# Constant products at phase boundaries, modulation products moved to the mixer's end, and interleaved Strassen products in a two-layer diffusion trunk on one core

## Chip, cores and metric

The kernel runs on one core of one Trainium2 chip (trn2). The metric is the device time of one execution in microseconds (us). The engines are named as in the profile: PE is TensorE's matmul queue and PEld its weight loads, DVE is VectorE, ACT is ScalarE, POOL is GpSimd and SP is SyncE, which issues the DMAs.

## What is computed

The trunk has two layers on 640 tokens (128 of a context, 512 of a latent grid). Each layer is a SwiGLU channel mixer, a token mixer (layer 0 a bidirectional gated recurrence, RG-LRU; layer 1 a multi-scale pooling), and a second SwiGLU, each between two RMS norms and with a shift, a scale and a gate that come from a conditioning vector by a product with `mod_w`:

```python
def _layer(x, mod, l, norm_g, ffn_w1, ffn_w3, ffn_w2, mixer):
    sh1, sc1, g1, sh2, sc2, g2, sh3, sc3, g3 = jnp.split(mod[:, None, :].astype(x.dtype), N_MOD, axis=-1)
    h = _modulate(_rmsnorm(x, norm_g[l, 0]), sh1, sc1)
    x = x + 0.5 * g1 * _rmsnorm(_swiglu(h, ffn_w1[l, 0], ffn_w3[l, 0], ffn_w2[l, 0]), norm_g[l, 1])
    h = _modulate(_rmsnorm(x, norm_g[l, 2]), sh2, sc2)
    y, st = mixer(h)
    x = x + g2 * _rmsnorm(y, norm_g[l, 3])
    h = _modulate(_rmsnorm(x, norm_g[l, 4]), sh3, sc3)
    x = x + 0.5 * g3 * _rmsnorm(_swiglu(h, ffn_w1[l, 1], ffn_w3[l, 1], ffn_w2[l, 1]), norm_g[l, 5])
    return x, st
```

The width is 1024, the SwiGLU's inner width 2816. In the recurrence, `r` and `i` are sigmoids of products of the convolved input with 128x128 blocks, `a = exp(-8 r softplus(-lam))`, and two scans run over the tokens, one in each direction; their sum times the gelu of a gate goes through `w_out`.

## The kernel before

**Numbers.** All large products are of f32 data. Each factor is split into a high and a low part of type fp32r, and one product is three passes (low·high, high·low, high·high). The split costs two instructions for each piece: an ACT copy (L136, L207) and a DVE subtraction (L137, L208); `split` takes another engine for the subtraction if it is given one.

**Seven products.** A SwiGLU's up-projections (`ffn_u`, `ffn_v`, 11 pairs of 128-column matrices, called b here, of which u and v belong to `w1` and `w3`) are done Strassen-like: seven products of half size stand for eight. `h_sums` makes the sums of quarters of the activations that they need (S1 to S4 beside A11, A12 and A22). One product is 12 matmuls of 128x320 (`prod`, L539, through `mmP`, L524). `seven_rest` does S2, S3, S1, A22 and S4 of one matrix; DVE adds each result to the running quarter (L550 after S2, L553 after S3, L556 after S1, L559 after A22, L562 after S4). S4 is accumulated onto the PSUM bank in which S1 already lies (`onto=True`), and so it cannot start before L556 has read that bank. The four first matrices of a phase have their A11 and A12 done earlier, in `ffn_start`, and only their other five products in `ffn_rest`.

**Down-projection.** `mmB` (L608) multiplies the gated results with `w2` or `w_out`; `block_B` does so for a pair of matrices and all five token tiles, `final` does the last ones and calls `close`, which adds the residual (`res_half` L395, `res_close` L403), makes the normed input of the next phase (`c_next`, L411 and L415) and transposes it (`c_t`, PE L489, evictions ACT L500 and DVE L498).

**Modulation.** `mod_gen` is a generator: each `mod_step` takes two 512 KB pieces of `mod_w` (tile mw, loaded by SP) and issues eight 32-column matmuls of f32 data into a PSUM bank of kind m (L271). After four such steps DVE copies the sum out (L279), and the next step puts it into columns (`mod_cols`, L319) or, for the gate, makes the rows G (PE L301, ACT L304). `mod_until` runs steps until a named part is done.

**Phases and order.** The phases are start, `ffn_rest(0,0)`, the recurrent mixer (`rg_start`, `rg_rest`) with its `final`, `ffn (0,2)`, `ffn (1,0)`, the pool mixer, `ffn (1,2)`; (l,s) is layer and place in it. Where the program says `with order()`, PE executes in the order of the code; in the recurrent mixer and its `final` a scheduler orders it. The other engines' orders come from the scheduler everywhere. Every engine executes its queue in that order. The mixer works chunk by chunk (c = 0..7, 128 channels): products L533, gate matrices L844, sigmoid L845, exp L864, tanh L866, square root L870, scan L883, sums L893 to L895, the split L208 of the result g; the gelu L891 belongs to the chunk before.

Of the kernel before, what the change touches and what calls it, by code (L numbers as in the profile page):

```python
# [83 lines left out]
class Kern:  # L84
# [103 lines left out]
    def get(self):  # L188
        while not self.made:
            assert self.make()  # L190
        return self.made.pop(0)
# [251 lines left out]
    def h_sums(self, ks, cols, second):  # L443
# [11 lines left out]
        self.h_put("A22", ks, cols, f22, self.nc.gpsimd)  # L455
        self.nc.gpsimd.tensor_tensor(f12, f12, s2, op=ALU.subtract)  # L456
        self.h_put("S4", ks, cols, f12)

    def c_t(self, tiles, l, s, plain, tag="q"):
# [9 lines left out]
        if not plain:  # L469
            if t * P + w <= HT:  # L470
                dst = lambda kk: self.F[0][kk // HK][:, kk % HK, sl]
            else:
# [11 lines left out]
                self.sums[t] = self.h_sums(slice(0, HK), sums, second)  # L484
# [50 lines left out]

    def bank(self, tag="q"):
        return self.p(tag)[:, 0:HT]

    def prod(self, out, h, **kw):  # L539
        self.mmP(out, h, self.get(), **kw)  # L540
        self.room = max(0, self.room - self.room_step)
        self.done(1, self.room)

    def seven_rest(self, u, s1, tag):
# [4 lines left out]
        self.prod(p6, "S2")  # L549
        V.tensor_add(c12, p6, s1)  # L550
        p7 = self.bank(tag)
# [13 lines left out]
    def seven(self, u):  # L565
# [5 lines left out]
        it = self.seven_rest(u, s1, "q")  # L571
        next(it)
# [59 lines left out]
    def close(self, product, l, s, nxt, first=False):  # L632
# [17 lines left out]
        for t in range(NT):  # L650
# [8 lines left out]
            if nxt:  # L659
                self.c_next(t)  # L660
                if t == (1 if first else 3):
                    with self.tc.high_priority(300):
                        self.c_t((0, 1), *nxt)
                elif t == (2 if first else 4):
                    with self.tc.high_priority(300):
                        self.c_t((2,), *nxt)
            else:
                self.store(t)
# [32 lines left out]
    def ffn_start(self, nxt, used):  # L701
# [5 lines left out]
        copy = lambda m: self.nc.scalar.activation(self.s1[m], self.c11[m], AF.Copy)  # L707
        for m in range(2):
# [19 lines left out]
    def ffn_rest(self, l, s, nxt):  # L728
        for b in range(2):
            u, v = self.ffn_uv(b)  # L730
            for m, x in enumerate((u, v)):
                for _ in self.seven_rest(x, self.s1[2 * b + m], "b" if b == 0 else "q"):
                    pass
                if m == 0:
                    self.ffn_u(u, self.c11[2 * b])
                else:
                    self.ffn_v(b, u, v, self.c11[2 * b + 1])
                self.mod_step()
# [198 lines left out]
    def rg_rest(self):  # L937
        gw = None
        for c in range(KC):
            if 0 < c < KC - 1:  # L940
# [4 lines left out]
                self.mod_step()  # L945
# [18 lines left out]
            self.mod_step()  # L964
# [199 lines left out]
    def run(self):  # L1164
# [59 lines left out]
        self.rg_rest()  # L1224
        n = self.final((4, 5, 6, 7), 0, 1, (0, 2, False))
# [101 lines left out]
```

## Time and profile before

| | |
|---|---|
| time, median of 3 runs | 2265.6 us (2264.69 to 2265.93) |
| profiled execution: its own time | 2267.01 us |
| its span | 2265.2 us |
| mean granted clock of TensorE, share of full | 0.967 |
| PE busy | 2107.5 us (93%) |
| PEld busy | 1907.6 us (84%) |
| DVE busy | 1683.7 us (74%) |
| ACT busy | 1013.5 us (45%) |
| POOL busy | 175.4 us (8%) |
| chain that ended last, by engine | PE 74%, DVE 14%, ACT 6% |

A busy share is an average over the span. PE is at work nearly all the time inside the SwiGLU phases, and idle mostly at the boundaries between phases and in the recurrent mixer. In a timeline row, the number in brackets is the time for which the engine stood idle ahead of the row, with the instruction that ended the wait.

### The profile page before, as it was taken

Reading aid. Unit: us, or ns where it says so; the run is one execution under the profiler, and the core shown is the slowest. Engines: PE = TensorE matmul, PEld = TensorE weight load, DVE = VectorE, ACT = ScalarE, POOL = GpSimd, SP = SyncE. Lnnn points to the kernel's source line nnn. Section 1 sums busy time; section 2 is a strip of 40 time slices with the busy share of each in tenths; the row PEclk is TensorE's granted clock in tenths of the full one; section 3 lists DMA queues with packets and bytes.
Section 4 is the critical chain, followed back from the end, with each engine's and each line's share of the span. In section 5 each row is a group of like instructions: output and inputs, shape, how many; then the busy total and the mean of one; then the engine's idle time right before and its main releaser. Section 6 shows DMA issues by size and latency. Waiting matters only on the chain.

```text
span 2265.2 us, 32719 instructions
## 1 busy us (share of the span) xinstructions
PE 2107.5 (93%) x13015; PEld 1907.6 (84%) x13015; DVE 1683.7 (74%) x2655; ACT 1013.5 (45%) x1739; POOL 175.4 (8%) x165
## 2 busy tenths in 40 slices
PE   6799999998899779999999799999997589999998
PEld 4788999987788669899998688898896589999997
DVE  5867777766878786777776867677776786787775
ACT  5443333356857654333334643233336754333332
POOL 1000000011111320000001400000002310000001
PEclk8899999998999999999999899999999799999999
DMA  8424422234432343342223433444334342222222
GB/s 288 154 98 149 149 75 94 75 113 162 158 112 93 121 170 105 131 149 75 94 75 103 170 132 138 150 156 153 138 117 144 111 160 102 76 87 75 93 75 93
DMA packets 72713, 278.26 MB, mean 123 GB/s; under 512 B 7392, under 2 KB 15600, under 8 KB 61296
## 3 DMA queue, kind: packets, MB, share of 16 engines
q1 hardware_dynamic: 72528, 276.16, 35.4%
q8 instruction: 102, 1.67, 0.3%
q14 instruction: 51, 0.42, 0.1%
q0 software_dynamic: 32, 0.01, 0.0%
HBM read 260.40 MB, written 15.74 MB: 122 GB/s over the span
## 4 chain that ended last, share of the span: by engine, by line
PE 74%; DVE 14%; ACT 6%; issue 3%; POOL 2%; DMA 1%; SPq 0%; POOLq 0%; DVEq 0%; ACTq 0%
PE q L524 42%; PE b L608 24%; PE m L271 2%; PE b L524 2%; DVE wp L137 2%; PE q L533 2%; DVE h L208 1%; POOL st L365 1%; DVE mw L403 1%; DVE h L883 1%; DVE wp L177 1%; ACT yacc L415 1%; POOL c L456 1%; DVE T L150 1%; DVE yacc L395 1%
## 5 line engine op out<-in xcount | busy, mean ns | idle before, releaser
L524 PE MATMUL q<-h,wp 128*128 128x320 f32 x6912 | 1043.3, 312 | 24.9 <-ACT h L207 16.0
L524 PEld LDWEIGHTS q<-h,wp 128*128 128x128 f32 x6912 | 1026.2, 190 | 45.5 <-ACT h L207 17.2
L608 PE MATMUL b<-wp,g 128*128 128x512 f32 x2880 | 668.7, 392 | 11.6 <-DVE g L208 10.5
L608 PEld LDWEIGHTS b<-wp,g 128*128 128x128 f32 x2880 | 538.7, 188 | 130.4 <-DVE g L208 13.1
L136 ACT ACTIVATE wp<-raw 128x512 fp32r<-128x512 f32 x440 | 269.2, 629 | 644.6 <-PE b L608 329.6
L137 DVE TENSOR_TENSOR wp<-raw,wp 128x512 fp32r<-128x512 f32 x440 | 300.5, 691 | 91.4 <-ACT wp L136 89.4
L618 DVE TENSOR_TENSOR yacc<-yacc,b 128x512 f32<-128x512 f32 x380 | 257.8, 684 | 139.8 <-PE b L608 139.0
L177 DVE TENSOR_TENSOR wp<-raw,wp 128x1024 fp32r<-128x1024 f32 x118 | 143.9, 1220 | 74.0 <-PE q L524 52.5
L174 ACT ACTIVATE wp<-raw 128x1024 fp32r<-128x1024 f32 x94 | 99.6, 1059 | 156.2 <-PE q L524 144.0
L395 POOL TENSOR_TENSOR yacc<-yacc,G 128x512 f32<-128x512 f32 x30 | 44.3, 1476 | 1320.5 <-ACT mhl L369 1320.4
L136 ACT ACTIVATE wp<-T 128x512 fp32r<-128x512 f32 x176 | 105.4, 624 | 83.8 <-PE q L524 80.6
L150 DVE TENSOR_TENSOR T<-raw 128x1024 f32<-128x1024 f32 x88 | 108.6, 1234 | 37.7 <-DMA raw<-in_w_dram 36.6
L533 PE MATMUL q<-h,wp 128*128 128x320 f32 x768 | 127.2, 322 | 9.7 <-ACT h L207 7.0
L533 PEld LDWEIGHTS q<-h,wp 128*128 128x128 f32 x768 | 120.3, 198 | 15.4 <-ACT h L207 8.0
L137 DVE TENSOR_TENSOR wp<-T,wp 128x512 fp32r<-128x512 f32 x176 | 118.0, 691 | 12.7 <-ACT wp L136 12.6
L524 PE MATMUL b<-h,wp 128*128 128x320 f32 x480 | 84.7, 336 | 26.7 <-DVE c L556 10.4
L524 PEld LDWEIGHTS b<-h,wp 128*128 128x128 f32 x480 | 78.8, 208 | 33.3 <-issue 14.1
L271 PE MATMUL m<-mw,csil 128*32 128x256 f32 x1024 | 71.4, 390 | 8.1 <-DMA mw<-in_mod_w_dram 8.1
L207 ACT ACTIVATE g<-c 128x1280 fp32r<-128x1280 f32 x44 | 56.2, 1278 | 45.5 <-DVE c L590 45.5
L208 DVE TENSOR_TENSOR g<-c,g 128x1280 fp32r<-128x1280 f32 x44 | 65.4, 1485 | 9.5 <-ACT g L207 9.4
L584 ACT ACTIVATE c<-c 128x960 f32<-128x960 f32 x44 | 44.0, 1000 | 43.1 <-DVE c L562 43.1
L152 DVE TENSOR_TENSOR raw<-raw,T 128x512 f32<-128x512 f32 x88 | 61.2, 695 | 0.1
(205 smaller groups left out, 1667.6 us busy)
## 6 DMA issues: line engine op xcount, KB each, us to landing
raw<-in_w_dram SPq DMA_DIRECT2D x88, 1024.0 KB, 4.8
mw<-in_mod_w_dram SPq DMA_DIRECT2D x130, 512.0 KB, 4.3
raw<-in_w_dram SPq DMA_DIRECT2D x88, 512.0 KB, 4.6
x_spill<-mw SPq DMA_DIRECT2D x25, 512.0 KB, 2.6
mw<-x_spill SPq DMA_DIRECT2D x25, 512.0 KB, 3.7
raw<-in_w_dram SPq DMA_DIRECT2D x32, 256.0 KB, 4.4
raw<-in_w_in_dram SPq DMA_DIRECT2D x16, 512.0 KB, 4.5
wp<-in_mod_w_dram SPq DMA_DIRECT2D x8, 512.0 KB, 9.3
```

What stands on the lines that cost most here:

```text
L136: nc.scalar.activation(w[:, 0:512], src, AF.Copy)
L137: V.tensor_sub(w[:, 512:D], src, w[:, 0:512].bitcast(F32))
L150: V.tensor_sub(T, raw[:, 512:1536], raw[:, 0:1024])
L174: nc.scalar.activation(wh, r, AF.Copy)
L177: V.tensor_sub(wl, r, wh.bitcast(F32))
L208: (engine or self.nc.vector).tensor_tensor(lo, src, hi.bitcast(F32), op=ALU.subtract)
L271: nc.tensor.matmul(ps[32 * j:32 * j + 32, 0:256], self.csil[:, k, :], w[:, j * 256:(j + 1) * 256], start=(k == 0), stop=(k == KC - 1), til ...
L395: (self.nc.vector if n else self.nc.gpsimd).tensor_tensor(y, y, self.G[(l, s)][:, v, n * 512:(n + 1) * 512], op=ALU.mult)
L524: self.nc.tensor.matmul(out, a, b[:, k], start=(start and not onto and k == first and n == 0), stop=(stop and k == last and n == 2), skip_ ...
L533: self.nc.tensor.matmul(out, a[:, sl], b[k // 2][:, k % 2, cols], start=(n == 0), stop=(n == 3 * KC - 1))
L608: nc.tensor.matmul(pb, a[:, ts_], b[:, ns], start=(c == 0), stop=(c == total - 1))
L618: nc.vector.tensor_add(y, y, pb)
```

## The change

Four edits:

- `warm(n)` issues n products of constants (the identity by 256 columns of the table of constants, f32) into a bank of kind m, which nobody reads. 43 of them: two ahead of tile 2's transposes at the plain closes of (0,0) and (1,0) and at the close of (0,2); five ahead of the first A11 in each `ffn_start`; 14 ahead of the pool mixer's first transposes and eight ahead of its tile 2's.
- In the recurrent mixer a chunk has up to three modulation steps: behind the next chunk's products (L945), behind the gate matrices (L951) and at the chunk's end (L964). The first goes, the second stays, the third stays for odd chunks only; what is left is done by `mod_until` ahead of `final`.
- In `ffn_rest`, S2 of the next of the four first matrices stands between A22 and S4 of the one before, after the modulation step; all four now use banks of kind b.
- In the start, the subtraction of A22's split and the last sum of `h_sums` (L456) go from POOL to DVE.

```diff
--- before.py
+++ after.py
@@ -185,10 +185,10 @@
         self.live += 1
         return True
-    def get(self):
-        while not self.made:
+    def get(self, at=0):
+        while len(self.made) <= at:
             assert self.make()
-        return self.made.pop(0)
+        return self.made.pop(at)
     def done(self, n=1, room=0):
@@ -440,7 +440,7 @@
         hi, lo = self.H[n]
         self.split(hi[:, ks, cols], lo[:, ks, cols], src, engine)
-    def h_sums(self, ks, cols, second):
+    def h_sums(self, ks, cols, second, aside=None):
         V = self.nc.vector
         f21, f22, s1, s2 = second
@@ -452,8 +452,8 @@
         V.tensor_sub(f11, f11, f21)
         self.h_put("S3", ks, cols, f11)
         self.h_put("S1", ks, cols, s1)
-        self.h_put("A22", ks, cols, f22, self.nc.gpsimd)
-        self.nc.gpsimd.tensor_tensor(f12, f12, s2, op=ALU.subtract)
+        self.h_put("A22", ks, cols, f22, aside)
+        (aside or V).tensor_tensor(f12, f12, s2, op=ALU.subtract)
         self.h_put("S4", ks, cols, f12)
     def c_t(self, tiles, l, s, plain, tag="q"):
@@ -481,7 +481,7 @@
                 else:
                     dst = lambda kk: self.f2[kk // HK][:, kk % HK, sums]
                     second = [x[:, :, sums] for x in self.f2]
-                self.sums[t] = self.h_sums(slice(0, HK), sums, second)
+                self.sums[t] = self.h_sums(slice(0, HK), sums, second, nc.gpsimd)
         for j in range(KC // n):
             pt = self.p(tag)
             for q in range(n):
@@ -533,21 +533,28 @@
                 self.nc.tensor.matmul(out, a[:, sl], b[k // 2][:, k % 2, cols], start=(n == 0), stop=(n == 3 * KC - 1))
                 n += 1
+    def warm(self, n):
+
+        pt = self.p("m")
+        for _ in range(n):
+            self.nc.tensor.matmul(pt[:, 0:256], self.col("ident"), self.cols[:, 0:256], start=True, stop=True)
+
     def bank(self, tag="q"):
         return self.p(tag)[:, 0:HT]
-    def prod(self, out, h, **kw):
-        self.mmP(out, h, self.get(), **kw)
+    def prod(self, out, h, at=0, **kw):
+        self.mmP(out, h, self.get(at), **kw)
         self.room = max(0, self.room - self.room_step)
         self.done(1, self.room)
-    def seven_rest(self, u, s1, tag):
+    def seven_rest(self, u, s1, tag, at=0):
         V = self.nc.vector
         c12, c21, c22 = u[:, 1, 0:HT], u[:, 0, HT:TOK], u[:, 1, HT:TOK]
         p6 = self.bank(tag)
-        self.prod(p6, "S2")
+        self.prod(p6, "S2", at)
         V.tensor_add(c12, p6, s1)
+        yield
         p7 = self.bank(tag)
         self.prod(p7, "S3")
         V.tensor_add(c21, p7, c12)
@@ -569,6 +576,7 @@
         s1 = u[:, 0, 0:HT]
         self.nc.scalar.activation(s1, p1, AF.Copy)
         it = self.seven_rest(u, s1, "q")
+        next(it)
         next(it)
         self.prod(p1, "A12", onto=True)
         next(it)
@@ -659,9 +667,13 @@
             if nxt:
                 self.c_next(t)
                 if t == (1 if first else 3):
+                    if first:
+                        self.warm(14)
                     with self.tc.high_priority(300):
                         self.c_t((0, 1), *nxt)
                 elif t == (2 if first else 4):
+                    if s != 1 or first:
+                        self.warm(8 if first else 2)
                     with self.tc.high_priority(300):
                         self.c_t((2,), *nxt)
             else:
@@ -705,6 +717,7 @@
         self.room, self.room_step = 6, 0
         self.done(used, self.room)
         copy = lambda m: self.nc.scalar.activation(self.s1[m], self.c11[m], AF.Copy)
+        self.warm(5)
         for m in range(2):
             self.prod(self.c11[m], "A11")
             copy(m)
@@ -726,16 +739,25 @@
         self.room_step = 1
     def ffn_rest(self, l, s, nxt):
-        for b in range(2):
-            u, v = self.ffn_uv(b)
-            for m, x in enumerate((u, v)):
-                for _ in self.seven_rest(x, self.s1[2 * b + m], "b" if b == 0 else "q"):
-                    pass
-                if m == 0:
-                    self.ffn_u(u, self.c11[2 * b])
+
+        last = None
+        for m in range(4):
+            if m % 2 == 0:
+                uv = self.ffn_uv(m // 2)
+            it = self.seven_rest(uv[m % 2], self.s1[m], "b", 1 if m else 0)
+            next(it)
+            if last:
+                last()
+            next(it)
+            self.mod_step()
+
+            def last(it=it, m=m, uv=uv):
+                next(it)
+                if m % 2 == 0:
+                    self.ffn_u(uv[0], self.c11[m])
                 else:
-                    self.ffn_v(b, u, v, self.c11[2 * b + 1])
-                self.mod_step()
+                    self.ffn_v(m // 2, *uv, self.c11[m])
+        last()
         self.new_y()
         self.block_B((0, 1), True)
         for b in range(2, NB):
@@ -942,7 +964,6 @@
                 self.rg_xr(c + 1, w, 0)
                 self.rg_xr(c + 1, w, 1)
                 self.done(2, 4)
-                self.mod_step()
             if c % 2 == 0:
                 gw = self.pair()
             self.rg_gm(c, gw)
@@ -961,7 +982,8 @@
                 self.rg_gate(c - 1, self.pair())
                 self.done(2, 4)
                 self.rg_y(c - 1)
-            self.mod_step()
+            if c % 2:
+                self.mod_step()
             if c == 3:
                 self.new_y()
                 self.g_on_dve = True
@@ -1222,6 +1244,8 @@
             n = self.ffn_rest(0, 0, (0, 1, True))
         self.rg_start((0, 1, True), n)
         self.rg_rest()
+        for m in self.phase_mods[0, 1]:
+            self.mod_until(*m)
         n = self.final((4, 5, 6, 7), 0, 1, (0, 2, False))
         with order():
             self.ffn_start((0, 2, False), n)
```

**PE at the end of the recurrent mixer.** The L533 rows are the last gate products of chunk 7, the L608 (after: L616) rows the first products with `w_out` of `final`. Before:

```order
L533 MATMUL q_6647<-h_4348,wp_6477 128x320
L533 MATMUL q_6647<-h_4352,wp_6357 128x320
L533 MATMUL q_6647<-h_4348,wp_6357 128x320
L608 MATMUL b_6699<-wp_6482,g_6204 128x512
L608 MATMUL b_6699<-wp_6530,g_6203 128x512
L608 MATMUL b_6699<-wp_6482,g_6203 128x512
```

After:

```order
L533 MATMUL q_6622<-h_4352,wp_6287 128x320
L533 MATMUL q_6622<-h_4348,wp_6287 128x320
L271 MATMUL m_6484<-mw_6588,csil_68 32x256 x4
L271 MATMUL m_6484<-mw_6594,csil_68 32x256 x4
L271 MATMUL m_6484<-mw_6678,csil_68 32x256 x4
L271 MATMUL m_6484<-mw_6684,csil_68 32x256 x4
L319 MATMUL b_6696<-cols_64,mrow_6694 128x8 x2
L616 MATMUL b_6702<-wp_6426,g_6122 128x512
L616 MATMUL b_6702<-wp_6474,g_6121 128x512
L616 MATMUL b_6702<-wp_6426,g_6121 128x512
```

Two modulation steps and the L319 that reads mrow now stand between the gate products and the first product with `w_out`.

**DVE at the same place, after.** L208 splits chunk 6's g, L915 to L917 (before: L893 to L895) sum chunk 7's scans, the second L208 splits chunk 7's g, L626 (before: L618) adds the first finished bank.

```order
L208 TENSOR_TENSOR g_6581<-h_4786,g_6580 128x640
L137 TENSOR_TENSOR wp_6665<-raw_6569,wp_6665 128x512
L915 TENSOR_TENSOR h_4789<-h_4789,h_4790 128x642
L279 COPY mrow_6694<-m_6484 128x256
L916 TENSOR_TENSOR h_4790<-h_4789,c_4792 128x512
L917 TENSOR_TENSOR h_4790<-h_4789,c_4792 128x128
L324 TENSOR_TENSOR ab_6478<-b_6696,cols_64 128x4x2 x2
L327 SCALAR_TENSOR_TENSOR ab_6478<-ab_6478,cols_64 128x16
L208 TENSOR_TENSOR g_6581<-h_4790,g_6580 128x640
L626 TENSOR_TENSOR yacc_5611<-yacc_5611,b_6702 128x512
```

The copy L279, L324 and L327 are new here; the rest stands in the order of before.

**DVE at the first two matrices of ffn (0,2).** c_7277 (after: c_7286) is the first matrix, c_7278 (after: c_7287) the second; L137, L150, L152 and L156 build weights. Before:

```order
L150 TENSOR_TENSOR T_7343<-raw_7292 128x1024
L556 TENSOR_TENSOR c_7277<-b_7325,c_7277 128x320
L152 TENSOR_TENSOR raw_7292<-raw_7292,T_7343 128x512
L559 TENSOR_TENSOR c_7277<-c_7277,b_7350 128x320
L156 TENSOR_TENSOR raw_7292<-raw_7292 128x512
L137 TENSOR_TENSOR wp_7346<-raw_7292,wp_7346 128x512
L137 TENSOR_TENSOR wp_7363<-T_7343,wp_7363 128x512
L137 TENSOR_TENSOR wp_7366<-T_7343,wp_7366 128x512
L137 TENSOR_TENSOR wp_7383<-raw_7292,wp_7383 128x512
L137 TENSOR_TENSOR wp_7386<-raw_7292,wp_7386 128x512
L562 TENSOR_TENSOR c_7277<-c_7277,b_7325 128x320
L150 TENSOR_TENSOR T_7420<-raw_7341 128x1024
```

After:

```order
L150 TENSOR_TENSOR T_7352<-raw_7301 128x1024
L563 TENSOR_TENSOR c_7286<-b_7334,c_7286 128x320
L152 TENSOR_TENSOR raw_7301<-raw_7301,T_7352 128x512
L566 TENSOR_TENSOR c_7286<-c_7286,b_7359 128x320
L156 TENSOR_TENSOR raw_7301<-raw_7301 128x512
L137 TENSOR_TENSOR wp_7355<-raw_7301,wp_7355 128x512
L137 TENSOR_TENSOR wp_7372<-T_7352,wp_7372 128x512
L137 TENSOR_TENSOR wp_7375<-T_7352,wp_7375 128x512
L137 TENSOR_TENSOR wp_7405<-raw_7301,wp_7405 128x512
L137 TENSOR_TENSOR wp_7408<-raw_7301,wp_7408 128x512
L556 TENSOR_TENSOR c_7287<-b_7391,yacc_7036 128x320
L150 TENSOR_TENSOR T_7427<-raw_7350 128x1024
```

The line numbers are shifted by 4 to 7 (L563 is L556 of before, L566 is L559). The second matrix's first sum, L550 of before (after: L556), now stands ahead of the next weight piece's L150, and still behind the five L137.

## Rows read from the trace of the kernel before

**Rows 1.** Waits of PE, whole span: engine, line, waited-for; us, times, longest.

```profile
PE b L524 <- DVE c L556: 10.4, 5, 4.1
...
PE q L524 <- DVE c L556: 6.2, 8, 1.2
```

**Rows 2.** Windows of 40 us: stretch; PE, PEld, DVE, ACT, POOL busy (instructions); clock, DMA share, GB/s.

```profile
800.00:840.00 40.00, 29.04 (x186) 25.22 (x186) 34.48 (x54) 21.17 (x35) 11.44 (x5) 0.91 0.50 177
```

**Rows 3.** Timeline of PE, first matrices of (0,2), one row of (1,0).

```profile
812.99 2.00 PE L524 MATMUL b<-h,wp 128*128 128x320 f32 x12 [2.75 <-DVE c L550]
819.13 3.54 PE L524 MATMUL b<-h,wp 128*128 128x320 f32 x12 [4.15 <-DVE c L556]
822.60 1.94 PE L271 MATMUL m<-mw,csil 128*32 128x256 f32 x16
...
834.17 1.07 PE L271 MATMUL m<-mw,csil 128*32 128x256 f32 x16
...
843.71 2.02 PE L524 MATMUL q<-h,wp 128*128 128x320 f32 x12 [1.23 <-DVE c L556]
...
1292.57 3.34 PE L524 MATMUL b<-h,wp 128*128 128x320 f32 x12 [3.53 <-DVE c L556]
```

**Rows 4.** Timeline of DVE, first matrices of (0,2).

```profile
818.51 0.48 DVE L556 TENSOR_TENSOR c<-b,c 128x320 f32<-128x320 f32 x1
...
823.52 0.47 DVE L562 TENSOR_TENSOR c<-c,b 128x320 f32<-128x320 f32 x1
```

**Rows 5.** Timeline of POOL and of DVE in the start.

```profile
53.24 2.64 POOL L208 TENSOR_TENSOR h<-g,h 128x640 fp32r<-128x640 f32 x1 [2.94 <-ACT h L207]
...
54.38 2.19 DVE L208 TENSOR_TENSOR h<-c,h 128x640 fp32r<-128x640 f32 x1
...
69.57 0.81 DVE L208 TENSOR_TENSOR h<-c,h 128x640 fp32r<-128x640 f32 x1
```

**Rows 6.** Timeline of PE, then ACT, inside the recurrent mixer.

```profile
577.61 0.64 PE L271 MATMUL m<-mw,csil 128*32 128x256 f32 x8 [3.42 <-DMA mw<-in_mod_w_dram]
...
580.24 3.54 PE L533 MATMUL q<-h,wp 128*128 128x320 f32 x12 [0.73 <-DVE wp L177]
...
549.82 1.28 ACT L845 ACT_TABLE_LOAD   x1
551.12 0.53 ACT L845 ACTIVATE h<-b,cols 128x322 f32<-128x322 f32 x1
```

**Rows 7.** Timeline of PE, then DVE, at the end of the recurrent mixer.

```profile
730.24 4.28 PE L608 MATMUL b<-wp,g 128*128 128x512 f32 x18
742.49 11.85 PE L608 MATMUL b<-wp,g 128*128 128x512 f32 x42 [7.97 <-DVE g L208]
...
742.96 0.82 DVE L893 TENSOR_TENSOR h<-h,h 128x642 f32<-128x642 f32 x1
...
747.55 2.08 DVE L618 TENSOR_TENSOR yacc<-yacc,b 128x512 f32<-128x512 f32 x3 [1.15 <-PE b L608]
```

**Rows 8.** Timeline of PE, then ACT, at the boundaries into (0,2) and (1,0).

```profile
776.98 0.42 PE L524 MATMUL q<-h,wp 128*128 128x320 f32 x1 [2.26 <-ACT h L207]
...
1249.37 6.70 PE L524 MATMUL q<-h,wp 128*128 128x320 f32 x24 [3.30 <-ACT h L207]
...
782.79 0.44 ACT L707 ACTIVATE yacc<-q 128x320 f32<-128x320 f32 x1 [0.71 <-PE q L524]
...
1256.11 0.44 ACT L707 ACTIVATE yacc<-q 128x320 f32<-128x320 f32 x1 [1.59 <-PE q L524]
```

**Rows 9.** Timeline of PE at the pool mixer's end.

```profile
1791.10 0.47 PE L489 MATMUL q<-cols,yacc 128*128 128x128 f32 x1 [5.25 <-ACT yacc L415]
1797.86 3.46 PE L489 MATMUL q<-cols,yacc 128*128 128x128 f32 x15 [6.29 <-ACT yacc L415]
1806.87 1.97 PE L489 MATMUL q<-cols,yacc 128*128 128x128 f32 x8 [5.54 <-ACT yacc L415]
1811.47 5.50 PE L524 MATMUL q<-h,wp 128*128 128x320 f32 x24 [2.64 <-ACT h L207]
```

## Prediction

> **What bounds the kernel now.** I read the page first: PE is busy for 93% of the span and the chain that ended last is PE for 74%, so time can be won only where PE stands idle or runs slowly. Next came the waits of PE. Two lines belong to edit three: PE waited 10.4 + 6.2 = 16.6 us, 13 times, for DVE's L556 ahead of a product S4 [rows 1]; the others that the change touches are waits for ACT at the boundaries and for DMA in the recurrent mixer. Then the windows: inside a SwiGLU a window of 40 us has PE busy nearly throughout, but 800 to 840 us has 29.0 of 40 at a granted clock of 0.91 [rows 2]. Last the timeline of such places. The reader is to see that an idle stretch costs twice: the same twelve products take 3.54 us behind a wait of 4.15 and 2.02 behind one of 1.23, and a modulation step 1.94 against 1.07 [rows 3]. The two durations are those of 1.2 and 2.4 GHz.
>
> **The interleaved first matrices.** Each of the 13 waits lies between A22 and S4. Of these S4 now has S2 of the next matrix ahead of it, and always the modulation step that stood behind it: 1.07 + some 1.9 us of ready work, or 1.07 alone for the fourth matrix. All waits but two are shorter than their cover: the longest in ordinary places is 1.23 [rows 3]. The two at a phase's first matrix, 4.15 and 3.53, leave 4.15 − 3.0 = 1.1 and 0.5. A new wait comes behind them: S1 of the second matrix needs the bank's sum by the second L550, which in DVE's new order stands behind the same five L137 that L562 stood behind. L562 began at 823.52 [rows 4], so L550 ends near 824.0, whereas PE, with S4 from 818.95 and S3 behind it, would reach that S1 at 822.7: 1.3 us. I put as much as 0.5 on the same place of (1,0). Left: 16.6 − 1.1 − 0.5 − 1.3 − 0.5 = 13.2. What the clock gives back: 3.54 − 2.02 and 1.94 − 1.07 in (0,2), 3.34 − 2.02 in (1,0) [rows 3], together 3.7, of which I take 2.3, since gaps remain. Sum **15.5 us**. Lower bound: where DVE is full, each wait only moves on to the next product, and half of the 16.6 stays: 8.3, said as 8. Upper: 16.6 + 3.7 = 20.3. The banks of kind b in place of q cost nothing: S1's is held for one product more, and the next use of that bank stands behind L562 with S3 between them.
>
> **The products of constants.** No row shows an f32 product with 128x128 weights and 256 columns. The nearest is L271: eight f32 products of 32x256 are issued in a step, four side by side, in 1.07 us at full and 1.94 at half clock [rows 3]. If four run together, one lasts 0.5 or 0.97 us, and that is the upper bound; if one after the other, 0.13 or 0.24. I take 0.5, as a full-width product can't share the array with another. Everything ahead of 1811 then fits into idle time: the 14 take 7.0 within 5.25 + 6.29, the eight 4.0 within 5.54, five 2.5 within 2.64 [rows 9], five within 3.30 and about as much as the 2.26 [rows 8]. At the plain closes ACT evicts the tile's transposes late anyway, which hides two products of 0.5.
>
> The gain: A11's 24 products took 6.70 in (1,0) [rows 8], where two times twelve at full clock take 4.0 [rows 3]. But what follows waits for ACT too, whose queue stood still for PE by 0.71 and 1.59 ahead of L707 [rows 8]. I take 1.1 at each of the two boundaries and 0.1 at the pool's, whose next transposes wait for ACT and not PE: **2.3 us**. Upper bound 0.71 + 1.59 + 0.7 = 3.0. Lower: at 0.97 with no further cover, 43 × 0.97 = 41.7 less the six waits named (5.25 + 6.29 + 5.54 + 2.64 + 2.26 + 3.30 = 25.3), a loss of 16.4.
>
> The Trainium skill (FP8 and Floating Point Precision, TensorE Precision Notes) counts four passes through the array for true FP32. With the 256/2.4 + 2.5 ns for a pass that the skill's TensorE: Matmul & The Clock Gate (Back-to-back issue gap) gives, that is an estimate of 0.44 us; the sum by it would be within 0.1 us of mine. No run so far shows such a product.
>
> **The start.** POOL's subtraction took 2.64 us, and a DVE subtraction beside it 2.19 where its twin took 0.81 [rows 5]: 1.4 lost on DVE. Three such meetings are in the start, 4.0 us; four operations more at 0.81 take 3.2 from it. DVE is 0.8 ahead, and A22's last piece is ready 2.64 − 0.81 = 1.8 sooner. PE waits for these pieces there, but also for ACT's halves: **1.5 us**, bounds 0 and 2.6.
>
> **The recurrent mixer until 730 us.** Modulation steps crowd early before: PE waits 3.42 for a piece of mod_w, twice more for less, and then does twelve products in 3.54 instead of 2.02 [rows 6]. The new order spreads the same steps over the chunks, which also moves the G rows from the busy chunks one and two to three. The second thing is ACT: in three chunks the scheduler put one sigmoid between two exps, a load to and fro [rows 6]; six of those loads are gone, 6 × 1.28 = 7.7 us of ACT. PE is nearly full in chunks four to seven, so only part of it counts: **6 us**, bounds 0 (the same transfers are waited for elsewhere) and 12 (7.7 + 3.42 + 1.5, rounded down).
>
> The Trainium skill (ScalarE: Activation LUTs, What ACT_TABLE_LOAD costs) adds a drain to the load, 2.66 us for a switch. The trace differs: the sigmoid starts at 551.12, 0.02 us behind the end of its load [rows 6]. By the page six loads would be 16.0 us.
>
> **The mixer's end.** Before, 18 products of `final` (4.28 us) were done from 730.24 on, while PE would else have waited for g until 742.49 [rows 7]. Now two steps and then L319 stand ahead of them in PE's queue. L319 waits for the copy L279, which stands on DVE behind the L893 of 742.96 to 743.78: 744.1 with the copy. Only then do the 18 begin, 4.28 us to 748.5, then nine for chunk six (2.2) and three for chunk seven (0.8): the first bank closes at 751.5 instead of 747.55. That is −4.0; L279, L324 and L327 on DVE ahead of chunk seven's g add up to 0.5: **−4.5 us**, bounds −6 (the steps' transfers late, at half clock) and 0 (DVE reaches L279 in an earlier gap).
>
> **Sum.** 15.5 + 2.3 + 1.5 + 6 − 4.5 = 20.8 us off the profiled execution's 2267.0: 2246.2. It is 1.4 above the median of the runs, so 2244.8, said as 2245.
>
> **Rivals.**
> - *The mixer gives nothing.* The waits for mod_w are due to the transfers, which queue with the weights and move along, and the end's loss stays whole. For it: PE is nearly full later on. Against: six loads go from ACT, whose results PE's gate products need. Gain 20.8 − 6 = 14.8: 2251.
> - *DVE, not the order, bounds the first matrices.* DVE was busy for 34.5 of 40 us at 800 to 840 [rows 2], and the waits reappear ahead of S1 and S3. Against: outside the two phase starts the waits were short. Gain 20.8 − 7.5: 2252.
> - *Constants at half clock, all in the way.* At 0.97 with the loss of 16.4: 2245 + 18.7 = 2263.5, about no change. For it: at the pool's end PE transposed 15 blocks in 3.46, a slow rate [rows 9], and the eight would take 7.8 against an idle 5.54. Against: idle PE also had to wait for the first of them.
> - *Slower: a constant product costs over 1 us.* The place is PE's queue ahead of the first real work of each phase. It breaks even at (18.5 + 25.3) / 43 = 1.02 us each; at 1.2 the loss is 26.3 and the time 2273. For it: a full-width f32 product with its weights is in no row. Against: the upper bound by L271 is 0.97. The Trainium skill (TensorE: Matmul & The Clock Gate, What overlaps and what doesn't) has matmuls start and end strictly in order, so a product that nobody reads does hold up one that is needed; no row here shows it for such products.
> - *Better:* the mixer at its upper bound, the end cheap, the clock fully back: 32 us off, 2233.
>
> **How the numbers follow.** The forecast has 0.56, with a range of its own from 2238 to 2252; the mixer without gain 0.13, DVE as the bound 0.10, constants in the way 0.08, slower 0.06, better 0.07. A measurement of this kernel can tell about 0.2% (4.5 us) from no change, so faster means below 2261: 0.56 + 0.13 + 0.10 + 0.07 = 0.86; same 0.08; slower 0.06. The range must leave out no more than 2 in 10: from 2231, which holds the better case, to 2260, which leaves out the two cases above it.
>
> **What the changed profile would show.** The waits on L556 fall from 16.6 to about 2 us, and one wait of about 1.3 for the second matrix's L550 appears in (0,2). The window that holds (0,2)'s first matrices has PE busy for some 5 us more. A constant product reads about 0.5 us, and A11 behind it runs at full clock. ACT has 38 table loads for 44. At the mixer's end PE waits for DVE's copy until chunk seven's sum and closes its first bank some 4 us later, counted from the last gate product. The prediction is wrong if that wait is far from 4 us, if the constants delay the transposes of the pool's tile 2, or if the L556 waits come back under another line's name.

## The result, and the profile after

The changed kernel takes 2240.6 us (median of 4 runs, 2237.93 to 2240.89) for 2265.5: the ratio is 0.9888, with a 95% interval from 0.9871 to 0.9905. That is 24.9 us, where 20.8 were forecast (2245). The profiled execution shows 26.6 by its spans (2265.2 to 2238.6).

To see where they come from, take the start times of the same instructions in the two traces. The last A12 product of the start ends 1.6 us sooner; (0,0)'s first products with `w2` start 4.1 sooner (118.02 and 113.89), so 2.5 lie in its first matrices. In the recurrent mixer the split L208 of chunk seven's g is 14.5 sooner (745.57 and 731.12), 10.3 more, or 10.2 counted from the mixer's first product (510.90 and 506.65); the first finished bank behind it only 9.6 (747.55 and 738.00), so 4.9 are lost again. Until (0,2)'s products with `w2` there are 15.7, until (1,0)'s 21.0, at the pool mixer's G rows 26.0, at the end 26.6.

The waits of PE, in the form of [rows 1]; L556 of this kernel is the first sum of a matrix (L550 of before), L563 the one that was L556. First two rows of before that [rows 1] doesn't have:

```profile
PE m L271 <- DMA mw<-in_mod_w_dram: 8.1, 7, 3.4
...
PE b L524 <- DVE c L550: 3.4, 2, 2.7
```

And after the change:

```profile
PE b L524 <- DVE c L556: 7.6, 5, 2.7
PE m L271 <- DMA mw<-in_mod_w_dram: 7.6, 3, 3.6
...
PE b L319 <- DVE mrow L279: 2.7, 1, 2.7
...
PE b L524 <- DVE c L563: 1.3, 2, 1.1
```

The 16.6 us for the sum behind S1 have become 1.3. A part has come back as waits for a matrix's first sum: 7.6 for 3.4. The waits for mod_w have become fewer, 7.6 in all for 8.1, but most of what is left has another place. Before, all of them lay between 556 and 627 us, inside the chunks. Now one does:

```profile
605.89 1.06 PE L271 MATMUL m<-mw,csil 128*32 128x256 f32 x2 [3.54 <-DMA mw<-in_mod_w_dram]
...
725.75 1.08 PE L271 MATMUL m<-mw,csil 128*32 128x256 f32 x8 [0.39 <-DMA mw<-in_mod_w_dram]
```

The second row, with one of 3.64 just ahead of it that is shown below, stands behind the last gate product. So ahead of that product the waits for mod_w went from 8.1 to 3.5.

The window of [rows 2], in which (0,2)'s first matrices now come some 9 us sooner:

```profile
800.00:840.00 40.00, 34.78 (x255) 31.17 (x253) 38.20 (x61) 18.52 (x30) 2.81 (x3) 1.00 0.57 191
```

PE is busy for 34.8 of 40 us where it was 29.0, at a granted clock of 1.00 where it was 0.91, while DVE, busy for 38.2, is nearly full. The timeline of PE at the place of [rows 3]:

```profile
803.79 2.00 PE L524 MATMUL b<-h,wp 128*128 128x320 f32 x12 [2.71 <-DVE c L556]
805.72 1.07 PE L271 MATMUL m<-mw,csil 128*32 128x256 f32 x16
806.72 2.03 PE L524 MATMUL b<-h,wp 128*128 128x320 f32 x12
809.84 3.76 PE L524 MATMUL b<-h,wp 128*128 128x320 f32 x24 [1.09 <-DVE c L563]
814.86 3.79 PE L524 MATMUL b<-h,wp 128*128 128x320 f32 x24 [1.25 <-DVE c L556]
```

The rows are A22, the modulation step, S2 of the second matrix, then S4 of the first with S3, then S1 with A22. What is left of the wait of 4.15 is 1.09, and the second matrix's first sum brings a new one of 1.25; all rows are at full clock, where S4 took 3.54 before.

ACT's table loads for the sigmoid and the exp, by groups of instructions (count, busy us, ns of one), before and then after:

```profile
L845 ACT ACT_TABLE_LOAD x14 | 18.0, 1283 | 0.3
L864 ACT ACT_TABLE_LOAD x13 | 16.7, 1283 | 0.2
...
L867 ACT ACT_TABLE_LOAD x11 | 14.1, 1283 | 0.2
L886 ACT ACT_TABLE_LOAD x10 | 12.8, 1283 | 0.2
```

With the others there are 38 for 44. DVE's waits for the sigmoid in the mixer, from 505 to 735 us, before and after:

```profile
DVE h L858 <- ACT h L845: 18.4, 6, 3.6
...
DVE h L880 <- ACT h L867: 4.7, 4, 2.9
```

Against these 13.7 us, one wait of 4.1 for PE is new on DVE. The end of the recurrent mixer, PE and then DVE, which answer to [rows 7]:

```profile
724.28 1.08 PE L271 MATMUL m<-mw,csil 128*32 128x256 f32 x8 [3.64 <-DMA mw<-in_mod_w_dram]
...
729.57 1.02 PE L319 MATMUL b<-cols,mrow 128*128 128x8 f32 x4 [2.73 <-DVE mrow L279]
730.44 9.79 PE L616 MATMUL b<-wp,g 128*128 128x512 f32 x34
```

```profile
728.36 0.82 DVE L915 TENSOR_TENSOR h<-h,h 128x642 f32<-128x642 f32 x1
729.09 0.42 DVE L279 COPY mrow<-m 128x256 f32<-128x256 f32 x1
...
731.12 0.83 DVE L208 TENSOR_TENSOR g<-h,g 128x640 fp32r<-128x640 f32 x1
738.00 0.69 DVE L626 TENSOR_TENSOR yacc<-yacc,b 128x512 f32<-128x512 f32 x1 [6.06 <-PE b L616]
```

PE stands ahead of L319 until DVE has come past L915 to the copy. L626 follows chunk seven's L208 after 6.88 us; before, L618 followed at 747.55, 1.98 us after this row:

```profile
745.57 0.82 DVE L208 TENSOR_TENSOR g<-h,g 128x640 fp32r<-128x640 f32 x1 [0.80 <-ACT g L207]
```

The constants at the pool mixer's end, to be laid beside [rows 9]. The profile lists two records for an f32 product, so x28 are 14 products:

```profile
1759.79 6.20 PE L540 MATMUL m<-cols 128*128 128x256 f32 x28
...
1771.95 3.46 PE L489 MATMUL q<-cols,yacc 128*128 128x128 f32 x15 [5.85 <-ACT yacc L415]
1775.21 3.71 PE L540 MATMUL m<-cols 128*128 128x256 f32 x16
1783.03 1.97 PE L489 MATMUL q<-cols,yacc 128*128 128x128 f32 x8 [4.11 <-ACT yacc L415]
1784.79 4.43 PE L540 MATMUL m<-cols 128*128 128x256 f32 x10
1788.70 4.04 PE L524 MATMUL q<-h,wp 128*128 128x320 f32 x24
```

One costs 6.20/14 = 0.44 us at full clock (granted 1.00 from 1760 to 1765.5), and 4.43/5 = 0.89 in the third row of them, which is mostly at half (0.50 from 1785 to 1788.6). Behind the first two rows of them PE still waits for ACT's L415; behind the five A11 starts with no wait, at most 0.8 us after ACT's split L207 (1787.17 to 1787.89). A11 takes 4.04 for 5.50. But from the 15 transposes to tile 2's there are now 11.1 us (1771.95 to 1783.03), and 9.0 before.

### The profile page after: what moved, and what is told of

The parts are those of the page before. It is cut to its first block, busy times and chain, and to the rows that moved or that the text cites. A ratio compares the mean times of both kernels' runs of the same rounds, so it can differ in the third digit from the quotient of the medians.

```text
span 2238.6 us, 32886 instructions
## 1 busy us (share of the span) xinstructions
PE 2115.5 (95%) x13101; PEld 1917.5 (86%) x13101; DVE 1682.8 (75%) x2659; ACT 1003.2 (45%) x1733; POOL 157.3 (7%) x161
## 4 chain that ended last, share of the span: by engine, by line
PE 78%; DVE 10%; ACT 5%; issue 3%; POOL 2%; DMA 1%; SPq 1%; POOLq 0%; DVEq 0%; ACTq 0%
PE q L524 40%; PE b L616 25%; PE b L524 5%; PE q L533 3%; PE m L271 2%; DVE wp L137 1%; DVE h L208 1%; DVE mw L403 1%; POOL st L365 1%; PE b L866 1%; POOL c L456 1%; ACT mhl L369 1%; DVE h L905 1%; ACT yacc L415 1%; PE b L301 1%
## 5 line engine op out<-in xcount | busy, mean ns | idle before, releaser
L524 PE MATMUL q<-h,wp 128*128 128x320 f32 x6432 | 965.5, 311 | 12.8 <-ACT h L207 9.1
L524 PEld LDWEIGHTS q<-h,wp 128*128 128x128 f32 x6432 | 952.9, 189 | 27.7 <-ACT h L207 10.1
L616 PE MATMUL b<-wp,g 128*128 128x512 f32 x2880 | 670.4, 393 | 4.5 <-DVE g L208 2.5
L616 PEld LDWEIGHTS b<-wp,g 128*128 128x128 f32 x2880 | 540.9, 189 | 123.3 <-DVE g L208 4.2
L626 DVE TENSOR_TENSOR yacc<-yacc,b 128x512 f32<-128x512 f32 x380 | 258.2, 685 | 146.1 <-PE b L616 145.2
L137 DVE TENSOR_TENSOR wp<-raw,wp 128x512 fp32r<-128x512 f32 x440 | 300.8, 692 | 82.6 <-ACT wp L136 80.6
L524 PE MATMUL b<-h,wp 128*128 128x320 f32 x960 | 156.5, 320 | 24.5 <-ACT h L207 9.9
L524 PEld LDWEIGHTS b<-h,wp 128*128 128x128 f32 x960 | 146.0, 194 | 37.1 <-ACT h L207 11.7
L150 DVE TENSOR_TENSOR T<-raw 128x1024 f32<-128x1024 f32 x88 | 108.7, 1236 | 37.7 <-DMA raw<-in_w_dram 36.7
L533 PE MATMUL q<-h,wp 128*128 128x320 f32 x768 | 123.9, 318 | 10.6 <-ACT h L207 7.0
L533 PEld LDWEIGHTS q<-h,wp 128*128 128x128 f32 x768 | 118.0, 195 | 15.0 <-ACT h L207 8.0
L137 DVE TENSOR_TENSOR wp<-T,wp 128x512 fp32r<-128x512 f32 x176 | 119.7, 704 | 10.9 <-ACT wp L136 10.8
L207 ACT ACTIVATE g<-c 128x1280 fp32r<-128x1280 f32 x44 | 56.3, 1279 | 43.0 <-DVE c L598 42.6
L208 DVE TENSOR_TENSOR g<-c,g 128x1280 fp32r<-128x1280 f32 x44 | 65.4, 1487 | 11.1 <-ACT g L207 11.0
L156 DVE TENSOR_TENSOR raw<-raw 128x512 f32<-128x512 f32 x88 | 61.5, 698 | 1.2
```

The costliest lines, as they stand in the source:

```text
L137: V.tensor_sub(w[:, 512:D], src, w[:, 0:512].bitcast(F32))
L150: V.tensor_sub(T, raw[:, 512:1536], raw[:, 0:1024])
L156: V.tensor_sub(t4, t2, b21)
L208: (engine or self.nc.vector).tensor_tensor(lo, src, hi.bitcast(F32), op=ALU.subtract)
L524: self.nc.tensor.matmul(out, a, b[:, k], start=(start and not onto and k == first and n == 0), stop=(stop and k == last and n == 2), skip_ ...
L533: self.nc.tensor.matmul(out, a[:, sl], b[k // 2][:, k % 2, cols], start=(n == 0), stop=(n == 3 * KC - 1))
```

## The experiments

**The interleaving alone.** The hunks of `get`, `prod`, `seven_rest`, `seven` and `ffn_rest` on the kernel before; the core is

```diff
+            it = self.seven_rest(uv[m % 2], self.s1[m], "b", 1 if m else 0)
+            next(it)
+            if last:
+                last()
+            next(it)
+            self.mod_step()
```

> The kernel before with the interleaved first matrices alone (all four in banks of kind b). Theory of the prediction: 15.5 us off, about 2250, and the waits on L556 fall from 16.6 to about 3. Rival, DVE bounds these places: 8 us off, about 2257, with as much waiting ahead of S1 and S3. Second rival, the gain came with the constant products, which keep the clock up at the start of these matrices: under 10 us without them.

It takes 2248.6 us for 2265.6: ratio 0.9927 (0.9912 to 0.9942), 17.0 us off. PE at the same place in (0,2):

```profile
816.63 3.75 PE L524 MATMUL b<-h,wp 128*128 128x320 f32 x24 [1.08 <-DVE c L557]
821.64 3.79 PE L524 MATMUL b<-h,wp 128*128 128x320 f32 x24 [1.25 <-DVE c L550]
```

The two remaining waits and the full clock are there with no constant in the kernel. From the last A12 row to the first product with `w2`, the four phases together are 16.8 us shorter in this trace. The waits for the two sums and the one between them fell from 20.0 to 7.5 us (5.9 for L550, 1.3 for L557, 0.3 for L554), so 12.5 are waits. The theory stands. Both rivals fall by their size, though waits ahead of S1, the sign of the first, did appear.

**The constants alone.** `warm` and its three places in the code on the kernel before.

```diff
+        self.warm(5)
         for m in range(2):
             self.prod(self.c11[m], "A11")
```

> The kernel before with the 43 products of constants alone. Theory of the prediction: 2.3 us off, about 2263, from A11 at full clock at the entries into (0,2) and (1,0), nothing at the pool's end. Rival, constants in the way: 2 to 16 us slower. Second rival, read from the changed kernel, where the pool mixer's stretch was 4.9 us shorter with nothing but two constant products ahead of it: then this run too has the pool mixer shorter by 3 to 5 us.

2265.0 us (10 runs) for 2265.6: ratio 0.9999 (0.9989 to 1.0009), no measurable difference. The pool mixer's stretch, from its first L1009 to the G rows, lasts 34.3 us for 38.7 before, so the third expectation holds; but of that 2.2 were lost again by the next A11, since tile 2's transposes come 11.1 us behind the 15. In this kernel the scheduler had put the five of (0,2) not ahead of A11 but into the idle stretch ahead of chunk seven's g, where they did nothing.

**The modulation edit alone.**

```diff
-                self.mod_step()
             if c % 2 == 0:
                 gw = self.pair()
...
-            self.mod_step()
+            if c % 2:
+                self.mod_step()
...
+        for m in self.phase_mods[0, 1]:
+            self.mod_until(*m)
```

> The kernel before with the modulation edit of the recurrent mixer alone. Theory of the prediction: 6 us gained until the last gate product, 4.5 lost behind it, 1.5 us off in all, about 2264. The changed kernel's trace rather says that chunk seven's scans begin 10 us sooner and 5 of them are lost: 5 us off, about 2260. Rival, the mixer gives nothing: 4 to 5 us slower, about 2270.

2258.8 us for 2265.6: ratio 0.9973 (0.9961 to 0.9985), 6.8 off, nearest to the second of the two theories. Chunk seven's g is 11.1 sooner, counted from the mixer's first product, and 4.5 of it are lost behind. The profiled execution shows more, 9.4 by the spans, and the rest lies where nothing was edited: in the pool mixer. Two of its rows before, in the order of the program 24 products of a tile each,

```profile
1757.75 5.46 PE L1009 MATMUL b<-wp,h 128*128 128x256 f32 x24 [1.75 <-DVE h L208]
...
1766.53 4.60 PE L1009 MATMUL b<-wp,h 128*128 128x256 f32 x24 [2.08 <-DVE h L208]
```

and in this run:

```profile
1750.74 4.61 PE L1009 MATMUL b<-wp,h 128*128 128x256 f32 x24 [2.33 <-DVE h L208]
...
1758.30 3.06 PE L1009 MATMUL b<-wp,h 128*128 128x256 f32 x24 [2.08 <-DVE h L208]
```

The same products, the second 24 behind the same wait of 2.08, run at another rate: the stretch lasts 34.9 us for 38.7, with a mean granted clock of 0.85 for 0.74. So the pool mixer moves by some 4 us where nothing was edited, most of it with the rate, and a gain seen there in one trace can't be put down to an edit.

**The start alone.**

```diff
-        self.h_put("A22", ks, cols, f22, self.nc.gpsimd)
-        self.nc.gpsimd.tensor_tensor(f12, f12, s2, op=ALU.subtract)
+        self.h_put("A22", ks, cols, f22, aside)
+        (aside or V).tensor_tensor(f12, f12, s2, op=ALU.subtract)
```

(`c_t` passes POOL as `aside`, the start nothing.)

> The kernel before with the start's two operations on DVE instead of POOL alone. Theory of the prediction: 1.5 us off (0 to 2.6), about 2264. Rival, PE waits for ACT's halves there anyway: no change.

2264.6 us (10 runs): ratio 0.9994 (0.9984 to 1.0003), not told apart from nothing. Its trace has the last A12 product end at 74.26 for 75.49, so 1.2 us are there at the place. The four alone come to 17.0 + 0.7 + 6.8 + 1.0 = 25.5 us and together to 24.9. With intervals of 2 to 4 us to either side on each of these numbers, that shows no action of one on another, and would not show one of a few us.

**The change without its constants.** `warm` returns at once.

> The changed kernel with no product of constants (everything else as changed). Theory of the prediction: 2.3 us slower than the changed kernel, about 2243. Theory after the first four runs: constants are worth nothing in sum, since they shorten the pool mixer by the clock and lose 2 us ahead of its tile 2 and 1 at the entry into (1,0): within 2 us of the changed kernel. Rival, the clock they keep up also serves the interleaved matrices: 5 us slower or more.

2242.4 us, ratio 0.9895 (0.9880 to 0.9910), 1.8 over the changed kernel with overlapping intervals. Two of its rows, A11 of (0,2) and tile 2's transposes at the pool's end:

```profile
768.28 5.17 PE L524 MATMUL q<-h,wp 128*128 128x320 f32 x23 [0.36 <-DVE h L208]
...
1784.66 1.97 PE L489 MATMUL q<-cols,yacc 128*128 128x128 f32 x8 [5.55 <-ACT yacc L415]
```

In the changed kernel the 23 products take 3.64 us, at full clock, 1.5 less; yet the products with `w2` start at 840.87 with constants and at 840.95 without. What A11 gains, the next transposes give back by waiting for ACT, 2.80 for 1.49. At the entry into (1,0) PE with constants starts A11 1.0 later, runs it no faster (6.36 for the last 23) and is 1.8 ahead only later, since it no longer waits twice for ACT's L415 (1.14 and 1.97 without them).

**The change without the 14.**

```diff
-                        self.warm(14)
+                        self.warm(0)
```

> The changed kernel without the 14 products ahead of the pool mixer's first transposes. Theory: they cost nothing on PE, but with them the scheduler put the sums of squares L369 of tile 2 on ACT behind the evictions and splits of tiles 0 and 1, and L415 of tile 2, for which PE waits, comes 2.1 us late; without them the distance from the 15 transposes to tile 2's is 9.0 us as before and not 11.1, and the kernel is 2 us faster, about 2238.5. Rival, PE's queue is what delays tile 2: no change in that distance, since eight products stay. Second rival, the 14 keep the clock up at A11: that product falls back to 5.5 us and eats the gain.

2238.0 us, ratio 0.9877 (0.9860 to 0.9893): 2.5 under the changed kernel by the medians, with overlapping intervals. The trace shows the place. DVE (the two halves of tile 2's residual, L403) and then ACT in the changed kernel, ahead of tile 2's L415:

```profile
1776.37 0.74 DVE L403 SCALAR_TENSOR_TENSOR mw<-yacc,st,mw 128x512 f32<-128x512 f32 x1
...
1779.90 0.74 DVE L403 SCALAR_TENSOR_TENSOR mw<-yacc,st,mw 128x512 f32<-128x512 f32 x1
...
1780.67 0.63 ACT L369 ACTIVATE yacc<-mw 128x512 f32<-128x512 f32 x1 [1.94 <-DVE mw L403]
...
1782.25 1.33 ACT L415 ACTIVATE yacc<-mw,st 128x512 f32<-128x512 f32 x2 [0.24 <-POOL st L365]
```

Before, these halves had another place in DVE's order:

```profile
1797.81 1.75 DVE L403 SCALAR_TENSOR_TENSOR mw<-yacc,st,mw 128x512 f32<-128x512 f32 x1 [0.44 <-POOL st L365]
...
1801.00 0.73 DVE L403 SCALAR_TENSOR_TENSOR mw<-yacc,st,mw 128x512 f32<-128x512 f32 x1
```

There the first half stood ahead of DVE's evictions L498, 0.72 us behind the start of tile 1's L415 on ACT (1797.09), and the second 3.91 behind it. In the changed kernel both stand behind the four evictions, the second behind two splits L208 as well: 5.19 and 8.72 behind (L415 at 1771.18). ACT's two L369 that square these halves moved too, and ACT stood idle for 1.94 us ahead of the second, waiting for DVE. Without the 14, DVE's order is that of before, and PE's transposes come at

```profile
1772.04 3.46 PE L489 MATMUL q<-cols,yacc 128*128 128x128 f32 x15 [6.28 <-ACT yacc L415]
...
1781.05 1.27 PE L489 MATMUL q<-cols,yacc 128*128 128x128 f32 x8 [1.83 <-ACT yacc L415]
```

9.0 us apart, with the eight products still in between. PE's queue was not the delay. The place that the theory named is right, the engine is not: ACT's order changed, but the wait that ended last was for DVE, on which the scheduler had put the residual behind the evictions. A11, at 3.64 us for its last 23 products, did not fall back to 5.5, so the second rival falls.

**No step left for the mixer's end.**

```diff
-            if c % 2:
+            if c % 2 or c > 3:
                 self.mod_step()
```

> The changed kernel with the modulation step at a chunk's end also for chunks four and six, so that no step is left for the mixer's end and the copy L279 stands on DVE ahead of chunk seven's scans. Theory: the 18 first products of the last projection start behind the last gate product again, the first bank closes 3 to 4.5 us sooner than in the changed kernel counted from chunk seven's scans, about 2237 in all. Rival, the two steps cost as much inside the chunks, where PE is nearly full: no change. Second rival, the scheduler splits sigmoid and exp again (40 table loads for 38): 2 to 3 us of the gain are lost.

2234.3 us, ratio 0.9862 (0.9847 to 0.9876): 6.3 under the changed kernel, with intervals that just meet. DVE at the end of the mixer:

```profile
730.56 0.83 DVE L208 TENSOR_TENSOR g<-h,g 128x640 fp32r<-128x640 f32 x1 [0.52 <-ACT g L207]
732.55 1.37 DVE L626 TENSOR_TENSOR yacc<-yacc,b 128x512 f32<-128x512 f32 x2 [1.17 <-PE b L616]
```

L626 follows L208 after 1.99 us, as it did before the change, and 4.9 sooner than in the changed kernel. The condition of the second rival holds, there are 40 loads, and its price is not seen: chunk seven's g is 1.8 us sooner than in the changed kernel, counted from the mixer's first product. With both last edits (without the 14, and so):

> Both edits together, without the 14 products and with the steps at the ends of chunks four and six. Theory: the two gains add, 5 to 6 us under the changed kernel, about 2235. Rival, either gives nothing: about 2238.

it is 2233.0 us, ratio 0.9855 (0.9840 to 0.9870): of the 2.5 only 1.3 show.

**Halves of the modulation edit.** On the kernel before, without the step behind the next chunk's products, but with that at every chunk's end:

```diff
                 self.done(2, 4)
-                self.mod_step()
             if c % 2 == 0:
```

> The kernel before with one half of the modulation edit: the step behind the next chunk's products goes, that at every chunk's end stays, nothing is left for the mixer's end. 38 table loads as in the changed kernel. Theory, six loads fewer on ACT are the mixer's gain: chunk seven's last split g comes some 10 us sooner as with the whole edit, and with no stall behind it the kernel is 10 us faster, about 2256. Rival, spreading the steps is the gain (no waits for pieces of mod_w, no G rows in busy chunks): most steps still come early here, so half of it or less, 2260 or more.

and the other way round:

```diff
-            self.mod_step()
+            if c % 2:
+                self.mod_step()
             if c == 3:
```

> The kernel before with the other half: the step at a chunk's end only for odd chunks, that behind the next chunk's products stays, nothing is left for the mixer's end. 38 table loads too. Theory, ACT's loads: about 2256 as well, and chunk seven's split 10 us sooner. Rival, the spreading: the steps are a little later than in the other half, so more than that one gains, but under the whole edit without its stall.

The first takes 2248.0 us for 2263.7, ratio 0.9927 (0.9913 to 0.9942), the second 2251.0, ratio 0.9944 (0.9927 to 0.9960): 15.7 and 12.7 off, each about twice what the whole edit is worth. Chunk seven's g is 15.7 and 12.4 us sooner, counted from the mixer's first product, and L618 follows it by 2.6 and 1.9. PE's waits from 505 to 735 us in the first half's run:

```profile
PE m L271 <- DMA mw<-in_mod_w_dram: 1.4, 1, 1.4
```

So both are well under the 2256 that the theories said. Counted from the mixer's first product to chunk seven's g, with the waits for mod_w that lie ahead of the last gate product:

| kernel | g sooner by | table loads | waits for mod_w |
|---|---|---|---|
| before | | 44 | 8.1 |
| modulation edit alone | 11.1 | 38 | 3.0 |
| changed kernel | 10.2 | 38 | 3.5 |
| no step left for the end | 12.0 | 40 | 3.4 |
| first half | 15.7 | 38 | 1.4 |
| other half | 12.4 | 38 | 0.7 |

With the edit alone another 5.1 us of such waits lie behind the last gate product, in the changed kernel 4.0. Every kernel has fewer loads and less waiting than before, but the gain follows neither the one nor the other from row to row. No run takes loads away and leaves the steps where they are, so how the gain divides is not shown. What is shown is that the spread chosen for the change is not the best: either half is worth about twice as much.

**The version that follows.** The changed kernel with the step at every chunk's end,

```diff
-            if c % 2:
-                self.mod_step()
+            self.mod_step()
```

> The changed kernel with the modulation step at every chunk's end, as in the half that was worth 15.7 us alone (two steps a chunk, none left for the mixer's end, 38 table loads). Theory: the last edit's gain of 6.8 becomes some 15.7, so 9 us under the changed kernel, about 2231.5. Rival, the clock in the pool mixer made up part of that difference: 5 to 6 us, about 2235, as with the steps at the ends of chunks four and six.

takes 2230.6 us, ratio 0.9850 (0.9835 to 0.9865), and without the 14

> The same without the 14 products of constants ahead of the pool mixer's first transposes. Theory: 2.5 us less again, about 2229, with tile 2's transposes 9.0 us behind the 15 ahead of them. Rival, no gain beside the other, since the clock at A11 falls: about 2231.5.

2227.6 us, ratio 0.9837 (0.9820 to 0.9853). The kernel before took 2264.5 beside these two, so they gain 33.8 and 36.9 us where the change gained 24.9: the last is 12 us ahead of the changed kernel. In the second run tile 2's transposes come 9.0 us behind the 15, in the first 11.1.

## Why the prediction was right

The time lay 4.4 us under the forecast, inside its own range from 2238 to 2252. The interleaving and the modulation edit are faster alone, as was said; the other two can't be told apart from nothing. The sum was short by 4.1 us (20.8 for 24.9). The mixer's term is 4.2 too small in the trace; that the smaller misses of the others about cancel is luck. By its steps:

- *The interleaved first matrices* (15.5): 17.0 alone. Of waits 12.5 went where 13.2 were put. The two waits that it worked out for (0,2), 1.1 for S4 and 1.3 for the second matrix's first sum, read 1.09 and 1.25. At (1,0) the latter was 1.22, where 0.5 was put. The clock gave back more than the 2.3: the rest of the 16.8 is 4.3, and no row of (0,2) above is at half clock any more. The rival, DVE as the bound, has its condition (38.2 of 40 us busy) and not its price. One reading was off without effect: the longest of the ordinary waits was not 1.23 but 1.68, in (0,0), still less than its cover.
- *The mixer's end* (−4.5): −4.9, told by the run with no step left there. The order was right: PE behind L319, L319 behind the copy, the copy behind L915. The wait itself reads 2.73 and not some 4, because PE stood 4.0 us for pieces of mod_w ahead of it.
- *The recurrent mixer until 730* (6): 10.2, and this is the term that was mis-sized, inside its bounds of 0 and 12. Two things went into it, and both went the way that was said. Six loads are gone from ACT, 7.7 us, of which only a part was let count because PE looked full. DVE, whose sums the next chunk needs, waited for the sigmoid 18.4 us before and 4.7 after. And the waits for mod_w ahead of the last gate product went from 8.1 to 3.5. So too little was taken of the two together; which of them brought how much stays open, as the table above has it. That the last steps' transfers would be late was within the bounds of the mixer's end; it cost nothing in this trace, since DVE's copy came later still (729.09, behind 726.83).
- *The products of constants* (2.3): 0.7 alone and 1.8 in the changed kernel, neither told apart from nothing. Their price, 0.44 and 0.89, was near the 0.5 and 0.97 taken as the upper bound, so the rival with over 1.02 us falls, as does the one with all of them in the way: they held a ready instruction for at most 0.9 us, where two of them stand ahead of tile 2's transposes at the close of (1,0) (1709.40 to 1710.27). Their gain came otherwise than was said. At (0,2) A11 ran at full clock and nothing came of it; at (1,0) it ran mostly at half clock all the same, and 1.8 came there by shorter waits for ACT; at the pool mixer, counted at 0.1, some 1.6 were won by the rate, which moves without any edit there, and as much lost by DVE's new order. That the transposes of the pool's tile 2 would be delayed was named as a sign against the prediction. They were, by 2.1 us, and by DVE's queue, at which it had not looked there.
- *The start* (1.5): 1.0 alone, with 1.2 at the place; inside its bounds, and below what the runs can tell.

By the Trainium skill (ScalarE: Activation LUTs, What ACT_TABLE_LOAD costs) a switch has a drain of 1.38 us beside the load; the trace shows 0.02 us between load and sigmoid. Six switches by the page are 16.0 us, by the rows 7.7, and the mixer gained 10.2, to which shorter waits for mod_w may have gone as well. No run sets the drain apart, so it isn't settled by that sum; in the rows it is not seen.

## What to carry to other kernels

An accumulation that waits for another engine is best parted from what it waits for by work of the next unit that is ready anyway, and the new first wait can be read from the in-order queue of the engine that makes the sums: at (0,2) it came out to a tenth of a microsecond. Work moved to a phase's end stands in front of the next phase on every queue it touches, and one copy behind a late instruction cost 4.9 us. Filler on one engine can also change what the scheduler does on the others: compare the orders of all engines, not only of the one that is filled, and follow a wait to the engine that ends it last.

## What was not expected of the hardware

The same 24 products of the pool mixer, both times behind a wait of 2.08 us for the same line, took 4.60 us in the kernel before and 3.06 with the modulation edit. PE is busy there for 25.3 of 38.7 us before, and the stretch lasts from 32.6 to 38.7 us over the fourteen traces of this study. Constants ahead of an idle stretch did not always go with the full rate behind it: 15 transposes took 3.46 us with 14 constants that ended 5.85 us ahead of them, and without them. Eight transposes took 1.97 with the eight constants that ended 4.1 us ahead and 1.27 in the run where only 1.83 us lay between.
